# S5 scan in segments, S5 states copied to contiguous rows, rotary and value steps moved between engines

## The chip, the cores and the metric

The kernel runs on 1 core of one Trainium2 chip. The metric is the device time of one execution in microseconds (us); the time of a kernel is the median of its runs. The engines are named as the profile names them: PE (TensorE matmuls), PEld (its weight loads), DVE (VectorE), ACT (ScalarE), POOL (GpSimd) and SP (SyncE, which issues all loads and stores here).

## The reference, cut to what matters

Two transformer-like blocks work on one sequence of 512 positions and 1024 features in fp32. The change lies in the second block: a projection into q, k, v, two gates and u, eight heads of retention with rotary positions, and an S5 branch, a linear recurrence over the 512 positions with 64 groups of 64 complex states.

```python
def second_block(x, mem, positions, norm1_g, w_in, ret_gn_g, s5_a_re, s5_a_im, s5_log_dt,
              s5_b_re, s5_b_im, s5_c_re, s5_c_im, s5_d, s5_glu_w, s5_glu_b, w_out,
              norm2_g, norm_mem_g, xa_wq, xa_wk, xa_wv, xa_wo, norm_f_g):
...
        h = rms_norm(x, norm1_g[l])
        proj = h @ w_in[l]
        q, k, v, g_ret, u, g_s5 = jnp.split(proj, SPLITS, axis=-1)
        q = rotary(q.reshape(B, L, RET_HEADS, RET_DK), positions)
        k = rotary(k.reshape(B, L, RET_HEADS, RET_DK), positions)
        v = v.reshape(B, L, RET_HEADS, RET_DV)
        ret = retention(q, k, v, ret_gn_g[l]).astype(x.dtype) * jax.nn.silu(g_ret)
        ssm = s5_branch(u, s5_a_re[l], s5_a_im[l], s5_log_dt[l], s5_b_re[l], s5_b_im[l],
                        s5_c_re[l], s5_c_im[l], s5_d[l], s5_glu_w[l],
                        s5_glu_b[l]).astype(x.dtype) * jax.nn.silu(g_s5)
        x = x + jnp.concatenate([ret, ssm], axis=-1) @ w_out[l]
...
def s5_branch(u, a_re, a_im, log_dt, b_re, b_im, c_re, c_im, d, glu_w, glu_b):
...
    def combine(e1, e2):
        a1r, a1i, b1r, b1i = e1
        a2r, a2i, b2r, b2i = e2
        return (a2r * a1r - a2i * a1i,
                a2r * a1i + a2i * a1r,
                a2r * b1r - a2i * b1i + b2r,
                a2r * b1i + a2i * b1r + b2i)

    _, _, xr, xi = lax.associative_scan(combine, (a_seq_re, a_seq_im, bu_re, bu_im), axis=1)
    y = (jnp.einsum('blgn,gpn->blgp', xr, c_re.astype(f32))
         - jnp.einsum('blgn,gpn->blgp', xi, c_im.astype(f32)))
    y = y.reshape(Bsz, L, W) + d.astype(f32) * uf
    y = jax.nn.gelu(y)
    y = y * jax.nn.sigmoid(y @ glu_w.astype(f32) + glu_b.astype(f32))
    return y
```

`rotary` swaps the two halves of each head's 64 features and combines them with cosine and sine; `retention` has a per-head normalisation of the 128 value features, whose mean the kernel takes off v beforehand.

## The kernel before

**Tiles and passes.** Activations lie transposed, 128 features in the partitions and 512 positions in the columns, eight tiles (KT = 8) for 1024 features. Each fp32 product is made of three passes in a rounded fp32 form (fp32r), high by high, low by high and high by low part, so a 128 x 128 piece of a weight costs three 128x512 matmuls. A weight tile goes through SP (load into `wr`), ACT (high part `wh`) and DVE (`wl` = `wr` - `wh`), two tiles ahead of the matmuls that use it. PSUM has six buffers `ps` for products and two `st` for everything short. 61 SBUF slots of 128x512 (`s` in the trace) are handed out by `A()` and given back by `F()`.

**What sets the order.** `ft` and `tf` are the weight jobs. `n.later(cost, f)` puts a piece of work on a background queue, and a job's `pump=` says how much of the queue goes out in the course of the job; `delay` puts a step off by some jobs. From this program order a scheduler makes the queue of each engine.

**The stretch around the change, in order of time.** (1) u jobs; `state_in` multiplies u by input matrices and ACT writes the results into `arr` [128, 128 chunks, 2, 32]: 128 chunks of four positions; real and imaginary parts; 32 columns, so the 128 chunks of one column lie 256 bytes apart. (2) The scan over the chunks, `step(c)`, c = 1..127: four DVE operations of 64 columns, each on the result of chunk c - 1, sent by `later`. (3) Eight q/k jobs with `ev_qk`: four DVE copies of 32 partitions swap the halves, one DVE product, and a product and a sum on POOL. (4) Two v jobs with `ev_v`: scaled copy on ACT, mean over 128 columns on DVE, subtraction on POOL. (5) A loop over eight heads with two gate jobs each, scores, value products, normalisation. (6) `s5_load(m)`, `s5_out(m)`, m = 0..7: for four column groups a product with `M` and two with `Cr`, `Ci` whose moving operand is read from `arr` with its 256-byte step; ACT takes the sum out and SP stores it to `Yd`. They run among the weight matmuls of `w_out`. (7) `s5_act` and eight glu jobs. Earlier, about 830 to 1100 us, `small` and its neighbours make the S5 tables (powers of the transition, `s5P`) beside other weight jobs.

Two view helpers, `cj` and `jc`, read a 512-column tile as 4 x 128 and 128 x 4; one of the two walks in steps of 16 bytes.

## Time and profile before

| | us |
|---|---|
| median of 3 runs (1859.61 to 1868.07) | 1859.93 |
| the profiled execution | 1861.86 |
| its span | 1860.1 |

| engine | busy us | share |
|---|---|---|
| PE | 1796.9 | 97% |
| PEld | 1480.5 | 80% |
| DVE | 1250.5 | 67% |
| ACT | 654.6 | 35% |
| POOL | 360.4 | 19% |

A page of the profile tells how long each engine was busy and what it waited for; a timeline lists instructions in order of start, equal neighbours put together (x4), and in brackets the idle time ahead of one and who ended it. Matmuls overlap, so the price of one is the distance from start to start, not its length. The clock column of a stretch is the granted TensorE clock as a share of full speed.

### The profile page before, as it was taken

What the parts mean: (1) busy time and instruction counts of PE and PEld (TensorE: products, weight loads), DVE (VectorE), ACT (ScalarE), POOL (GpSimd) and SP (SyncE); (2) the same over time, 40 slices, a digit from 0 to 9 for tenths busy, and PEclk for the clock granted to TensorE, in tenths of its full rate; (3) what the DMA queues carried; (4) which work ended last, traced back from release to release, by engine and by line L of the source; (5) the groups of instructions that cost most, each with busy time, mean ns of one, the idle gap of its engine ahead of it and who ended that gap; (6) DMA issues with size and microseconds to landing.
All of it is one profiled execution on the core that took longest, in us unless ns stands there. A gap on an engine that the chain in (4) does not pass through costs nothing.

```text
span 1860.1 us, 22090 instructions
## 1 busy us (share of the span) xinstructions
PE 1796.9 (97%) x8242; PEld 1480.5 (80%) x8242; DVE 1250.5 (67%) x2242; ACT 654.6 (35%) x891; POOL 360.4 (19%) x316
## 2 busy tenths in 40 slices
PE   5999999999999998999998999999998999999997
PEld 4888888888877887788876888888876778888886
DVE  7888634478999999767443434476599993356644
ACT  4322223333387522424321222334322222354442
POOL 2000001130000000234436963024231010012102
PEclk9999999999999999999999999999998999999999
DMA  8788433233322223235656352454622225653211
GB/s 318 299 318 316 144 111 102 85 119 131 102 80 80 91 94 114 87 129 175 190 151 190 126 198 90 163 173 90 208 70 77 80 86 172 191 158 124 87 46 57
DMA packets 105356, 261.48 MB, mean 141 GB/s; under 512 B 15008, under 2 KB 32032, under 8 KB 105120
## 3 DMA queue, kind: packets, MB, share of 16 engines
q1 hardware_dynamic: 105248, 260.07, 42.6%
q8 instruction: 64, 1.05, 0.2%
q14 instruction: 44, 0.36, 0.1%
HBM read 239.19 MB, written 20.84 MB: 140 GB/s over the span
## 4 chain that ended last, share of the span: by engine, by line
PE 59%; issue 16%; DVE 11%; POOL 6%; DMA 6%; ACT 2%; SPq 1%; DVEq 0%; POOLq 0%; ACTq 0%
PE ps L152 54%; POOL s L133 5%; PE st L152 4%; DVE s L136 3%; DVE wl L133 2%; DVE arr L133 1%; DMA s<-Fd 1%; DVE s L133 1%; DVE st L133 1%; ACT s L147 1%; DMA wr<-in_ffn_w_gate 1%; DMA s<-in_s_bt_im 1%; DVE s L1464 1%; SPq L130 1%; DMA s<-in_s_bt_re 1%
## 5 line engine op out<-in xcount | busy, mean ns | idle before, releaser
L152 PE MATMUL ps<-s,wh 128*128 128x512 f32 (+1 forms) x4272 | 1321.0, 391 | 9.8 <-ACT wh L147 4.9
L152 PEld LDWEIGHTS ps<-s,wh 128*128 128x128 f32 x4272 | 800.5, 189 | 180.1 <-ACT wh L147 7.1
L152 PE MATMUL ps<-s,wl 128*128 128x512 f32 (+1 forms) x2136 | 830.6, 389 | 2.7 <-DVE wl L133 2.7
L147 ACT ACTIVATE wh<-wr 128x1024 fp32r<-128x1024 f32 (+1 forms) x277 | 289.5, 1047 | 834.1 <-PE ps L152 523.8
L133 DVE TENSOR_TENSOR wl<-wr,wh 128x1024 fp32r<-128x1024 f32 (+1 forms) x277 | 357.8, 1292 | 202.1 <-ACT wh L147 199.0
L152 PEld LDWEIGHTS ps<-s,wl 128*128 128x128 f32 x2136 | 402.3, 188 | 87.4 <-DVE wl L133 4.5
L133 POOL TENSOR_TENSOR s<-s,s 128x512 f32<-128x512 f32 (+2 forms) x168 | 232.6, 1389 | 708.0 <-DVE s L136 347.0
L133 DVE TENSOR_TENSOR s<-s,s 128x512 fp32r<-128x512 f32 (+3 forms) x249 | 199.3, 809 | 54.1 <-ACT s L147 52.5
L147 ACT ACTIVATE s<-s 128x512 fp32r<-128x512 f32 (+3 forms) x246 | 153.5, 637 | 224.7 <-DVE s L133 135.4
L152 PE MATMUL ps<-s,s 128*128 128x512 f32 (+7 forms) x648 | 152.5, 386 | 27.8 <-ACT s L147 19.3
L136 DVE SCALAR_TENSOR_TENSOR s<-s,ccw,s 128x503 f32<-128x503 f32 (+27 forms) x240 | 163.2, 735 | 0.7
L152 PEld LDWEIGHTS ps<-s,s 128*128 128x128 f32 (+2 forms) x648 | 108.4, 179 | 66.1 <-issue 22.7
L133 DVE TENSOR_TENSOR s<-s,ps 128x512 f32<-128x512 f32 (+1 forms) x61 | 40.7, 669 | 139.8 <-PE ps L152 139.6
L136 DVE SCALAR_TENSOR_TENSOR s<-ps,c,s 128x512 f32<-128x512 f32 x56 | 41.9, 748 | 83.5 <-PE ps L152 83.2
L389 DVE SCALAR_TENSOR_TENSOR ar<-ar,silc 128x1024 f32<-128x1024 f32 x72 | 89.2, 1251 | 10.2 <-DMA ar<-in_ada_w 9.7
L147 ACT ACTIVATE s<-ps 128x512 f32<-128x512 f32 (+1 forms) x115 | 66.2, 586 | 10.4 <-PE ps L152 10.3
L133 DVE TENSOR_TENSOR arr<-arr,st 128x64 f32<-128x64 f32 x254 | 63.2, 249 | 3.8
L133 DVE TENSOR_TENSOR s<-ps,s 128x512 f32<-128x512 f32 (+4 forms) x80 | 46.6, 615 | 24.6 <-PE ps L152 24.3
L133 DVE TENSOR_TENSOR s<-s,st 128x512 f32<-128x512 f32 x73 | 46.6, 680 | 14.4 <-PE st L273 13.9
L133 DVE TENSOR_TENSOR st<-arr,a 128x64 f32<-128x64 f32 x254 | 52.5, 245 | 3.6
L284 POOL TENSOR_TENSOR ls<-ls,mhalf 128x4 f32<-128x4 f32 x4 | 4.1, 1024 | 257.3 <-DVE ls L136 257.3
L133 POOL TENSOR_TENSOR s<-s 128x256 f32<-128x256 f32 x1 | 0.8, 846 | 246.8 <-ACT s L147 246.8
(155 smaller groups left out, 954.1 us busy)
## 6 DMA issues: line engine op xcount, KB each, us to landing
wr<-in_w_in SPq DMA_DIRECT2D x80, 512.0 KB
ar<-in_ada_w SPq DMA_DIRECT2D x72, 512.0 KB
wr<-in_ffn_w_gate SPq DMA_DIRECT2D x44, 512.0 KB
wr<-in_ffn_w_up SPq DMA_DIRECT2D x44, 512.0 KB
wr<-in_ffn_w_down SPq DMA_DIRECT2D x32, 512.0 KB
s<-Cd SPq DMA_DIRECT2D x32, 256.0 KB
wr<-in_w_out SPq DMA_DIRECT2D x16, 512.0 KB
wr<-in_ffn_w_down SPq DMA_DIRECT2D x16, 384.0 KB
```

Source lines behind the costliest of these rows:

```text
L130: self.nc.sync.dma_start(out=out, in_=in_)
L133: (eng or self.nc.vector).tensor_tensor(out=out, in0=a, in1=b, op=op)
L136: self.nc.vector.scalar_tensor_tensor(out=out, in0=a, scalar=s, in1=b, op0=op0, op1=op1)
L147: self.nc.scalar.activation(out=out, in_=in_, func=f, scale=scale)
L152: self.nc.tensor.matmul(out, lhsT=lhsT, rhs=rhs, start=start, stop=stop)
L284: self.nc.gpsimd.tensor_tensor(out=out, in0=v, in1=self.mhalf[:, 0:n], op=ALU.pow)
L389: n.nc.vector.scalar_tensor_tensor(out=w, in0=w, scalar=1.0, in1=n.silc, op0=ALU.mult, op1=ALU.mult, accum_out=n.mod[:, j:j + 1])
L1464: nc.vector.tensor_copy(out=s[b * 32:(b + 1) * 32], in_=ps[(b ^ 1) * 32:((b ^ 1) + 1) * 32])
```

## The change

The scan is done over 16 segments of eight chunks: seven steps inside all segments at once (in two halves of 512 columns), 15 short steps that carry the last chunk of one segment to that of the next, and seven steps that add the carried state to the other chunks (512 and 448 columns). Each step is four DVE operations with a slot as its temporary, so 508 operations become 172. The factors are powers 4, 8, .. 32 of the transition, made in `small` (`q4r`, `q4i`). `s5_load` copies the states of one m by two ACT operations into two slots with contiguous rows, and `s5_out` reads those, so an m holds six slots for four. The rotary copies go from DVE to ACT and the two POOL operations to DVE; the values' scaling, mean and subtraction are done by DVE from PSUM, without ACT and POOL. The pump amounts of the three kinds of jobs rise. `ccw` becomes a slot that is given back, and `mean_h` a column of `means`.

```diff
+    means = n.C([128, 2], name="means")
+    n.mean1, n.mean_h = means[:, 0:1], means[:, 1:2]
     nc.vector.memset(n.mean1, 1.0 / 1024)
+    nc.vector.memset(n.mean_h, 1.0 / 128)
...
-    n.ccw = n.C([128, 248], name="ccw")
-    n.ts(n.ccw, n.vecs[:, CCW_AT * 8:(CCW_AT + 31) * 8], 0.5)
+    n.ccw = n.A()
+    n.ts(n.ccw[:, 0:248], n.vecs[:, CCW_AT * 8:(CCW_AT + 31) * 8], 0.5)
...
+        n.F(n.ccw)
...
+        n.q4r, n.q4i = n.C([128, 8, 32], name="q4"), n.C([128, 8, 2, 32], name="q4i")
+        Q = n.q4r, n.q4i[:, :, 1, :]
+        for j in range(2):
+            nc.vector.tensor_copy(out=Q[j][:, 0, :], in_=P[j][:, 4, :])
+        s3 = n.A()
+        t3 = s3[:, 0:128].rearrange("p (k q) -> p k q", k=4)
+        for w in (1, 2, 4):
+            b = [Q[j][:, w - 1, :].unsqueeze(1).to_broadcast([128, w, 32]) for j in range(2)]
+            cmul(n, Q[0][:, w:2 * w, :], Q[1][:, w:2 * w, :], Q[0][:, 0:w, :], Q[1][:, 0:w, :], b[0], b[1], t3[:, 0:w, :])
+        n.F(s3)
+        n.ts(n.q4i[:, :, 0, :], Q[1], -1.0)
...
-        a8 = [n.C([128, 2, 32], name="a8") for _ in range(2)]
-        for j in range(2):
-            nc.vector.tensor_copy(out=a8[0][:, j, :], in_=n.s5P[0][:, 4, :])
-        n.ts(a8[1][:, 0, :], n.s5P[1][:, 4, :], -1.0)
-        nc.vector.tensor_copy(out=a8[1][:, 1, :], in_=n.s5P[1][:, 4, :])
-        G["a8"] = a8
-        G["tmp"] = [n.C([128, 2, 32], name="st") for _ in range(2)]
...
-            for c in range(1, 128):
-                n.later(0.55, step(c))
-
-    def step(c):
-        def f():
-            arr, a8, tmp = G["arr"], G["a8"], G["tmp"]
-            p = arr[:, c - 1]
-            n.tt(tmp[0], p, a8[0], ALU.mult)
-            n.tt(tmp[1], p[:, ::-1, :], a8[1], ALU.mult)
-            n.tt(arr[:, c], arr[:, c], tmp[0], ALU.add)
-            n.tt(arr[:, c], arr[:, c], tmp[1], ALU.add)
-        return f
+            scan()
+
+
+
+    def scan():
+        x = G["arr"].rearrange("p (s i) r q -> p s i r q", i=8)
+
+        def add(dst, src, i, w):
+            def f():
+                s = n.A()
+                t = s[:, 0:w * 64].rearrange("p (s r q) -> p s r q", s=w, r=2)
+                re = n.q4r[:, i].unsqueeze(1).unsqueeze(1).to_broadcast([128, w, 2, 32])
+                im = n.q4i[:, i].unsqueeze(1).to_broadcast([128, w, 2, 32])
+                n.tt(t, src, re, ALU.mult)
+                n.tt(dst, dst, t, ALU.add)
+                n.tt(t, src[:, :, ::-1, :], im, ALU.mult)
+                n.tt(dst, dst, t, ALU.add)
+                n.F(s)
+            return f
+
+        for i in range(1, 8):
+            for h in (slice(0, 8), slice(8, 16)):
+                n.later(2.8, add(x[:, h, i], x[:, h, i - 1], 0, 8))
+        for s in range(1, 16):
+            n.later(1.0, add(x[:, s:s + 1, 7], x[:, s - 1:s, 7], 7, 1))
+        for i in range(7):
+            for lo, hi in ((1, 9), (9, 16)):
+                n.later(2.8, add(x[:, lo:hi, i], x[:, lo - 1:hi - 1, 7], i, hi - lo))
...
+        for r in range(2):
+            x = n.A()
+            n.act(x.rearrange("p (a c) -> p a c", a=4), G["arr"][:, :, r, m * 4:m * 4 + 4].rearrange("p c a -> p a c"), AF.Copy)
+            t.append(x)
...
-        U, M, Cr, Ci = G.pop(("s5", m))
-        arr = G["arr"]
+        U, M, Cr, Ci, Xr, Xi = G.pop(("s5", m))
         ps = n.ST()
         for c in range(4):
             x = slice(c * 128, (c + 1) * 128)
             n.mm(ps[:, x], M[:, x], U[:, x], True, False)
-            for r, w in enumerate((Cr, Ci)):
-                n.mm(ps[:, c * 128 + 1:(c + 1) * 128], w[:, x], arr[:, 0:127, r, m * 4 + c], False, r == 1)
+            for r, (w, s) in enumerate(((Cr, Xr), (Ci, Xi))):
+                n.mm(ps[:, c * 128 + 1:(c + 1) * 128], w[:, x], s[:, c * 128:c * 128 + 127], False, r == 1)
         n.act(U, ps, AF.Copy)
         n.load(Yd[m], U)
-        n.F(U, M, Cr, Ci)
+        n.F(U, M, Cr, Ci, Xr, Xi)
...
             for b in range(4):
-                nc.vector.tensor_copy(out=s[b * 32:(b + 1) * 32], in_=ps[(b ^ 1) * 32:((b ^ 1) + 1) * 32])
+                n.act(s[b * 32:(b + 1) * 32], ps[(b ^ 1) * 32:((b ^ 1) + 1) * 32], AF.Copy)
             t = n.A()
             n.tt(t, ps, n.cos, ALU.mult)
-            n.tt(s, s, n.sin, ALU.mult, nc.gpsimd)
-            n.tt(t, t, s, ALU.add, nc.gpsimd)
+            n.tt(s, s, n.sin, ALU.mult)
+            n.tt(t, t, s, ALU.add)
...
-        n.ft([(w2[m], KT)], X, ev_qk(m), pump=0.6)
+        n.ft([(w2[m], KT)], X, ev_qk(m), pump=2.0)
...
-                n.act(v, pss[t], AF.Copy, scale=r1.r[:, t:t + 1])
                 mu = n.C([128, 4], name="mu")
-                v4 = v.rearrange("p (h e) -> p h e", h=4)
-                nc.vector.reduce_sum(out=mu, in_=v4, axis=AX.X)
-                n.ts(mu, mu, 1.0 / 128)
-                n.tt(v4, v4, mu.unsqueeze(2).to_broadcast([128, 4, 128]), ALU.subtract, nc.gpsimd)
+                ps4, v4 = (x.rearrange("p (h e) -> p h e", h=4) for x in (pss[t], v))
+                nc.vector.reduce_sum(out=mu, in_=ps4, axis=AX.X)
+                n.ts(mu, mu, r1.r[:, t:t + 1], 1.0 / 128, ALU.mult, ALU.mult)
+                n.stt(v4, ps4, r1.r[:, t:t + 1], mu.unsqueeze(2).to_broadcast([128, 4, 128]), ALU.mult, ALU.subtract)
...
-        tf(n, [a["w_v_2"][half, i] for i in range(4)], X, 4, ev_v(half), pump=2.0)
+        tf(n, [a["w_v_2"][half, i] for i in range(4)], X, 4, ev_v(half), pump=9.0)
...
-            n.ft([(w2[(8, 24)[j] + m], KT)], X, ev_g(j, m), pump=3.0)
+            n.ft([(w2[(8, 24)[j] + m], KT)], X, ev_g(j, m), pump=3.5)
```

DVE, at the second and third q/k job (`ps` a job's result, `s` slots, `st`, `a` and `arr` the scan's). Before:

```order
L133 TENSOR_TENSOR wl_9997<-wr_9994,wh_9996 128x1024
L1464 COPY s_10025<-ps_10000 32x512 x3
L133 TENSOR_TENSOR s_10030<-ps_10000,s_6465 128x512
L133 TENSOR_TENSOR wl_10055<-wr_10052,wh_10054 128x1024
L1464 COPY s_10083<-ps_10058 32x512 x4
L133 TENSOR_TENSOR s_10088<-ps_10058,s_6465 128x512
L133 TENSOR_TENSOR wl_10107<-wr_10104,wh_10106 128x1024
L133 TENSOR_TENSOR st_9520<-arr,a_9514 128x64
L133 TENSOR_TENSOR st_9521<-arr,a_9515 128x64
L133 TENSOR_TENSOR arr<-arr,st_9520 128x64
L133 TENSOR_TENSOR arr<-arr,st_9521 128x64
```

Now, at the third q/k job (`q` and `q4i` are the scan's new factors):

```order
L133 TENSOR_TENSOR wl_10122<-wr_10119,wh_10121 128x1024
L133 TENSOR_TENSOR s_10103<-ps_10073,s_6464 128x512
L133 TENSOR_TENSOR s_10098<-s_10098,s_6465 128x512
L133 TENSOR_TENSOR s_10159<-arr,q_6605 128x512
L133 TENSOR_TENSOR s_10103<-s_10103,s_10098 128x512
L133 TENSOR_TENSOR arr<-arr,s_10159 128x8x64
L133 TENSOR_TENSOR s_10204<-arr,q_6605 128x512
L133 TENSOR_TENSOR s_10159<-arr,q4i_6606 128x512
L133 TENSOR_TENSOR arr<-arr,s_10204 128x8x64
L133 TENSOR_TENSOR arr<-arr,s_10159 128x8x64
L133 TENSOR_TENSOR wl_10167<-wr_10164,wh_10166 128x1024
```

The copies are gone from this queue, product and sum of the rotary stand in it, and the scan, which begins after the third job's product in both, is made of operations 512 columns wide.

ACT, from the last head's split to the S5 outputs (`st` are S5 sums that go out, `arr` the states). Before:

```order
L147 ACTIVATE s_11893<-s_11724 128x512
L147 ACTIVATE s_12001<-st_12025 128x512
L147 ACTIVATE s_12009<-st_12048 128x512
L147 ACTIVATE s_12070<-s_11882 128x512
L147 ACTIVATE s_12040<-st_12082 128x512
L147 ACTIVATE s_12074<-st_12105 128x512
```

Now:

```order
L147 ACTIVATE s_11696<-s_11561 128x512
L147 ACTIVATE s_11723<-arr 128x512
L147 ACTIVATE s_11725<-arr 128x512
L147 ACTIVATE s_11735<-arr 128x512
L147 ACTIVATE s_11737<-arr 128x512
L147 ACTIVATE s_11770<-arr 128x512
L147 ACTIVATE s_11772<-arr 128x512
L147 ACTIVATE s_11808<-arr 128x512
L147 ACTIVATE s_11715<-st_11747 128x512
L147 ACTIVATE s_11810<-arr 128x512
```

Seven copies of states stand ahead of the first sum, where before the first sums followed one another.

PE, first S5 output (`ps` with `wh`, `wl` is `w_out`; `st` the S5 sum). Before:

```order
L152 MATMUL st_12025<-s_12001,s_12002 128x128
L152 MATMUL ps_12195<-s_11262,wh_11741 128x512
L152 MATMUL ps_12195<-s_11261,wl_11742 128x512
L152 MATMUL st_12025<-arr,s_12003 128x127
L152 MATMUL ps_12195<-s_11419,wh_11741 128x512
L152 MATMUL ps_12195<-s_11420,wh_11741 128x512
L152 MATMUL ps_12195<-s_11419,wl_11742 128x512
L152 MATMUL st_12025<-arr,s_12004 128x127
L152 MATMUL st_12025<-s_12001,s_12002 128x128
L152 MATMUL st_12025<-arr,s_12003 128x127
L152 MATMUL st_12025<-arr,s_12004 128x127
```

Now:

```order
L152 MATMUL ps_12014<-s_11046,wh_11643 128x512
L152 MATMUL ps_12014<-s_11047,wh_11643 128x512
L152 MATMUL ps_12014<-s_11046,wl_11644 128x512
L152 MATMUL ps_12014<-s_11190,wh_11643 128x512
L152 MATMUL ps_12014<-s_11191,wh_11643 128x512
L152 MATMUL st_11747<-s_11723,s_11717 128x127
L152 MATMUL st_11774<-s_11727,s_11728 128x128
L152 MATMUL st_11747<-s_11725,s_11718 128x127
L152 MATMUL st_11747<-s_11715,s_11716 128x128
L152 MATMUL st_11747<-s_11723,s_11717 128x127
L152 MATMUL st_11747<-s_11725,s_11718 128x127
```

The second operand comes from a slot instead of `arr`, and 15 weight matmuls, of which the last five are shown, stand between the first product with M and the first with the states, where before there were two.

## Rows read from the trace of the kernel before

**Rows 1.** Page, first part: busy time, share of span, instructions of each engine.
```profile
PE 1796.9 (97%) x8242; PEld 1480.5 (80%) x8242; DVE 1250.5 (67%) x2242; ACT 654.6 (35%) x891; POOL 360.4 (19%) x316
```

**Rows 2.** Stretches: length, busy PE, PEld, DVE, ACT, POOL, clock, DMA share, GB/s.
```profile
1324.00:1367.75 43.75, 43.75 (x219) 37.08 (x217) 39.65 (x65) 11.76 (x15) 18.73 (x12) 1.00 0.26 90
1367.75:1419.98 52.23, 47.87 (x193) 38.03 (x192) 50.07 (x158) 13.20 (x16) 12.94 (x9) 0.93 0.24 81
1419.98:1453.86 33.88, 27.50 (x106) 19.92 (x104) 32.23 (x128) 6.90 (x9) 4.16 (x4) 0.85 0.25 86
1453.86:1565.97 112.11, 112.11 (x506) 86.09 (x506) 91.64 (x324) 33.28 (x48) 10.77 (x7) 1.00 0.29 95
1565.97:1606.08 40.11, 40.10 (x219) 37.54 (x218) 4.90 (x7) 6.40 (x10) 1.01 (x1) 1.00 0.65 211
```

**Rows 3.** Timeline, PE: start, length, instructions, idle before and its releaser.
```profile
1365.71 0.61 PE L152 MATMUL ps<-s,wh 128*128 128x512 f32 x2
...
1366.39 0.61 PE L152 MATMUL ps<-s,wh 128*128 128x512 f32 x2
...
1376.13 0.50 PE L152 MATMUL ps<-wl,s 128*128 128x512 f32 x1 [1.82 <-DVE wl L133]
...
1407.84 0.50 PE L152 MATMUL ps<-wl,s 128*128 128x512 f32 x1 [2.33 <-DVE wl L133]
...
1439.98 4.60 PE L152 MATMUL ps<-s,s 128*128 128x512 f32 x8 [6.38 <-DVE s L133]
```

**Rows 4.** Timeline, PE: 128-column matmuls from contiguous rows, then from the state array.
```profile
1315.34 7.48 PE L152 MATMUL st<-s,s 128*128 128x128 f32 x64
1322.57 0.47 PE L152 MATMUL ps<-s,wl 128*128 128x512 f32 x1
...
1583.78 1.03 PE L152 MATMUL st<-arr,s 128*128 128x127 f32 x4
1584.63 0.40 PE L152 MATMUL st<-s,s 128*128 128x128 f32 x2
```

**Rows 5.** Timeline, DVE, in the q/k jobs and in the first head round.
```profile
1366.71 1.81 DVE L133 TENSOR_TENSOR wl<-wr,wh 128x1024 fp32r<-128x1024 f32 x1
1368.45 1.44 DVE L133 TENSOR_TENSOR st<-arr,a 128x64 f32<-128x64 f32 x2
...
1370.32 0.36 DVE L133 TENSOR_TENSOR st<-arr,a 128x64 f32<-128x64 f32 x2
...
1440.74 1.21 DVE L133 TENSOR_TENSOR wl<-wr,wh 128x1024 fp32r<-128x1024 f32 x1
```

**Rows 6.** Timeline, POOL, beside the first of those.
```profile
1366.15 3.52 POOL L133 TENSOR_TENSOR s<-s,s 128x512 f32<-128x512 f32 x2 [3.78 <-DVE s L1464]
```

**Rows 7.** Groups by shape, DVE, 1287 to 1570: count, busy us, mean ns.
```profile
L133 DVE TENSOR_TENSOR arr<-arr,st 128x64 f32<-128x64 f32 x254 | 63.2, 249 | 3.8
L133 DVE TENSOR_TENSOR st<-arr,a 128x64 f32<-128x64 f32 x254 | 52.5, 245 | 3.6
...
L1464 DVE COPY s<-ps 32x512 f32<-32x512 f32 x32 | 22.0, 687 | 16.7 <-PE ps L152 16.2
L1486 DVE TENSOR_REDUCE mu<-s 128x4 f32<-128x512 f32 x8 | 5.4, 678 | 0.0
```

**Rows 8.** Timeline, DVE: 512 contiguous columns, then 512 with 16-byte steps (`jc`, `cj`).
```profile
1289.64 1.29 DVE L133 TENSOR_TENSOR s<-s,s 128x512 f32<-128x512 f32 x2
1290.85 4.94 DVE L133 TENSOR_TENSOR s<-ps,s 128x512 f32<-128x512 f32 x5
```

**Rows 9.** Groups by shape, ACT, 1287 to 1570, then 1606 to 1640.
```profile
L147 ACT ACTIVATE arr<-st 128x512 f32<-128x512 f32 x16 | 9.6, 597 | 18.9 <-PE st L152 18.9
...
L147 ACT ACTIVATE s<-s 128x512 f32<-128x512 f32 x8 | 9.0, 1122 | 10.5 <-DVE s L136 10.5
...
L147 ACT ACTIVATE s<-st 128x512 f32<-128x512 f32 x1 | 0.6, 598 | 3.5 <-PE st L152 3.5
```

**Rows 10.** Timeline, PE, while the S5 tables are made.
```profile
1014.62 0.73 PE L152 MATMUL ps<-s,wh 128*128 128x512 f32 x2 [2.63 <-ACT wh L147]
```

More of the change, by code (lines that the diff above doesn't have):

```diff
@@ L373, in setup @@
     nc.vector.memset(n.ones_est, 1.0 / (128 * LN.EST))
-    n.mean1 = n.C([128, 1], name="mean1")
+    means = n.C([128, 2], name="means")
+    n.mean1, n.mean_h = means[:, 0:1], means[:, 1:2]
     nc.vector.memset(n.mean1, 1.0 / 1024)
+    nc.vector.memset(n.mean_h, 1.0 / 128)
     n.mhalf = n.C([128, 32], name="mhalf")
@@ L1318, in second_block @@
     r1 = Rms(n)
-    n.mean_h = n.C([128, 1], name="meanh")
-    nc.vector.memset(n.mean_h, 1.0 / 128)
     Ud = n.DT([8, 2, 4, 64, 128], "Ud")
```

## The prediction

> **What bounds the kernel now.** I read the page first: PE is busy for 97% of the span [rows 1], so a change counts only where it takes work from PE, takes a stall from PE, or makes one. The 512-column matmuls follow one another at 0.68 us for three, 0.227 each [rows 3]; that is the floor of the weight jobs. Then I read the stretches of the second block one by one [rows 2]. In three of them PE is full (q/k jobs, later head rounds, S5 outputs); in the v jobs (52.23 us) and in the 33.88 us behind them it is not, and the clock column falls to 0.93 and 0.85. The v jobs hold 192 matmuls: 192 x 0.227 = 43.6, so 8.6 us are lost. Their timeline shows where [rows 3]: PE waits 1.82 and 2.33 us for `wl`, a weight's low part from DVE, and runs on slowly. In the first head round it waits 6.38 us for DVE, and the eight matmuls behind that take 4.60 us where eight at the steady rate take 1.8: 6.4 + 2.8 = 9.2. Together 17.8 us.
>
> Why DVE is late: it is busy 39.65 of 43.75, 50.07 of 52.23 and 32.23 of 33.88 us [rows 2]. It carries the scan (508 operations, 115.7 us), 22.0 us of rotary copies [rows 7], and it is slowed while POOL works: beside a POOL pair of 3.52 us [rows 6] `wl` takes 1.81 us and two scan operations 1.44, alone 1.21 and 0.36 [rows 5]. In the later head rounds DVE has slack again (91.64 of 112.11).
>
> The last place is the S5 outputs. There PE is full, yet its work is dear: 64 matmuls of 128 columns from contiguous rows take 1322.57 - 1315.34 = 7.23 us, 0.113 each; four from `arr`, with its 256-byte step, take 1584.63 - 1583.78 = 0.85, 0.2125 each [rows 4].
>
> **S5 operands contiguous.** 128 instructions go from 0.2125 to 0.113: 128 x 0.0995 = **-12.7 us**, all on PE, in a stretch in which PE never waits. The DMAs stay: at 211 GB/s and a share of 0.65 over 40.1 us [rows 2] they would take 0.65 x 40.1 = 26 us at full share, against 27.4 us that the stretch then has, so loads are about to bind too and cover less.
>
> **The copies that pay for it.** Sixteen ACT copies read `arr` with the step. No row shows this very operation. From below: ACT spread 512 columns from PSUM into `arr` in 0.597. From above: the GELU of `s5_act`, which writes in 16-byte steps, takes 1.122 [rows 9]. ACT has room for either (6.40 us of 40 used), but its order puts seven copies ahead of the first S5 sum and four more ahead of the second, while there are two `st` buffers, so the normalisation's next product waits for the first sum and the third S5 output for the second. The copies also need the whole scan: eight of its wide operations stand behind the last gate job's `wl`, near the start of the S5 outputs, and the 15 weight matmuls that now stand there cover all but about 1 us.
> - At 1.12: the first sum is out 7 x 1.12 + 0.6 = 8.4 us after the scan. PE begins after two copies (2.2) and has two outputs of 24 x 0.113 = 2.7 to do, so it is through at 7.6 and waits 0.8. The second sum is out at 8.4 + 4 x 1.12 + 0.6 = 13.5, PE is there at about 9.5: 4 us. With 1 us for the scan and some 2 us of slow matmuls behind such a wait (the 2.8 above is one case), 8 us.
> - At 0.60: sums at 4.8 and 7.8, PE through at 6.6 and 7.2: under 1 us, with the scan's wait 2 us.
>
> I take **+6**: the upper price is nearer by its kind of access, SBUF in small steps, but weight matmuls may fill part of the wait. So this half of the change is worth about -7.
>
> The Trainium skill ("SBUF — State Buffer", Specifications) says that SBUF is read in 16-byte lines and that each cross to a new line pays a penalty, which speaks against the copies: the step does not go away, ACT walks it now. The matmul prices of [rows 4] agree with it. By the page the copies cost like the GELU and the term is +8; without it +2.
>
> **Rotary, values and scan.** What leaves DVE: 32 copies, 22.0 us, and 508 narrow operations, 115.7 us [rows 7]. What comes: 16 operations for the rotary and 8 for the values at 0.645 (512 contiguous columns, 1.29 for two [rows 8]), 15.5 us; the scan in 112 wide operations at 0.645 and 60 narrow at 0.18 [rows 5], 72 + 11 = 83 us. POOL's q/k and v work goes away, and with it the slow `wl`. But more of the scan is pumped early: 56 of the 112 wide operations now lie before the end of the v jobs. DVE then has there: 56 x 0.645 = 36, 24 new operations 15.5, 21 `wl` at 1.21 = 25, the products of the eight q/k jobs 5, eight reductions of 0.678 [rows 7] and their small steps about 7: 89 us against 87.3 us of PE (43.75 + 43.6). So DVE is about as full as PE, no longer behind by 17.8. What lateness is left is covered by the two weight tiles that are prepared ahead (2 x 24 x 0.227 = 10.9 us). I take a rest of **+2** (0 to 5) and so **-15.8** in place of -17.8. ACT gets 32 copies: at about 0.6 each 19 us on top of 11.76 in 43.75 us; it keeps room. In the head rounds the rest of the scan, about 56 wide and 55 narrow operations, 46 us, takes the place of what was left of the old one; PE kept full there with DVE at 91.64 of 112.11.
>
> **Small edits.** The new table operations (24 against 4) are short, some 4 us of DVE at about 840 us, where PE has other weight jobs. But two hundred us later PE does wait on weights whose loads stand behind the tables' loads on SP (2.63 us at 1014.62 [rows 10], and a like one before): shifts of that order may move it either way. I take **0**, -3 to +5. `ccw` as a slot and `means` cost nothing: neither lies on a wait. The glu jobs begin sooner after the last S5 output and may wait for `s5_act`: 0, up to +2.
>
> **The sum.** 1861.86 - 12.7 + 6 - 15.8 + 0 = 1839.4 for the profiled execution. It stood 1.93 us above the median, so the forecast is about **1838 us**.
>
> **Rivals.**
> - *The copies cost the lower price and the ring hides them*: +2 instead of +6, 1834. For it: PSUM read with a step cost ACT nothing extra (0.597). Chance 0.14.
> - *Not the step makes the matmuls of `arr` dear*, but what stays, their 127 columns or the output that begins one column late. Then -12.7 is gone, and with it most of the wait for copies, PE being slower: 1838 + 12.7 - 4 = 1847. Against it: the two kinds differ in the operand above all. 0.08.
> - *DVE stays the bound.* The wide operations read segments 2 KB apart, one operand repeated, one reversed. If they cost what 512 columns in 16-byte steps cost, 4.94 for five = 0.99 [rows 8], the 56 early ones add 56 x 0.345 = 19 us of DVE, and with the 2 us it was behind PE loses what it loses now: 1861.86 - 1.9 - 12.7 + 6 - 17.8 + 21 = 1856, no change. Against it: inside a segment 64 columns are contiguous, and the narrow operation has the same reversal at 0.18. 0.10.
> - *Slower: the same place at a higher price.* To come out over 0.5% slower the stalls there must reach 34 us, so 32 us more on 56 operations, 0.57 each: from 1.22 us per wide operation. The nearest thing would be that each of the eight 64-column pieces costs like a narrow operation, 8 x 0.18 = 1.44; then 56 x 0.8 = 45 and 1861.86 - 1.9 - 12.7 + 6 - 17.8 + 47 = 1882. Nothing in the rows shows such a price per piece. 0.05.
> - *A new stall of over 10 us elsewhere* (tables, slots, six per m now): 1852 or so. 0.05.
>
> **How the numbers follow.** The forecast has 0.58. The best ends of all terms together: -12.7 + 2 - 17.8 - 3 = -31.5, 1828; the worst without a rival: -12.7 + 8 - 17.8 + 5 + 5 + 2 = -10.5, 1850. From 1829 to 1850 lie the forecast and the first two rivals, 0.80. This kernel can be told from no change at about 0.5%, so faster means under 1850.6: 0.80; within: 0.15; slower: 0.05.
>
> **What the profile will show.** S5: matmuls from slots at 0.113 each; copies of `arr` between 0.6 and 1.12 on ACT, with PE waits for them in the first three outputs only. Q/k and v: clock column 1.00, DVE about 90% busy, `wl` at 1.2 throughout, wide operations at 0.65. If the wide operations stand at 1.0 and PE waits for `wl`, the third rival holds. The forecast fails if matmuls from slots stay at 0.21, if the scan ends so late that the copies start well after the first product with M, or if the table stretch loses more than 5 us.

## The result

The changed kernel took 1841.97 us (median of 4 runs, 1838.59 to 1847.32) against 1860.72 before (4 runs): 18.75 us less, faster by 1.0%, a ratio of 0.9898 with a 95% interval of 0.988 to 0.9916. The forecast was 1838, the range 1829 to 1850. Its profiled execution happened to be the slowest of the four, 1847.32 us with a span of 1845.5.

### The profile page after: what moved, and what is told of

Read it like the earlier page. It is cut to its first block, busy times and chain, and to the rows that moved or that the text cites. A ratio compares the mean times of both kernels' runs of the same rounds, so it can differ in the third digit from the quotient of the medians.

```text
span 1845.5 us, 21756 instructions
## 1 busy us (share of the span) xinstructions
PE 1784.5 (97%) x8242; PEld 1469.6 (80%) x8242; DVE 1219.0 (66%) x1915; ACT 682.9 (37%) x931; POOL 322.7 (17%) x292
## 4 chain that ended last, share of the span: by engine, by line
PE 78%; POOL 7%; DMA 6%; DVE 4%; ACT 2%; issue 2%; SPq 1%; DVEq 0%; POOLq 0%; ACTq 0%
PE ps L152 75%; POOL s L133 6%; PE st L152 3%; DMA s<-in_s_bt_im 2%; DVE s L133 1%; ACT s L147 1%; SPq L130 1%; DMA s<-in_s_bt_re 1%; DVE ar L391 1%; DVE s L136 1%; DMA wr<-in_ffn_w_down 1%; DMA s<-Fd 1%; DMA wr<-in_ffn_w_gate 1%; DVE wl L133 0%; POOL s L143 0%
## 5 line engine op out<-in xcount | busy, mean ns | idle before, releaser
L152 PE MATMUL ps<-s,wh 128*128 128x512 f32 (+1 forms) x4272 | 1324.3, 392 | 11.7 <-ACT wh L147 6.6
L133 DVE TENSOR_TENSOR wl<-wr,wh 128x1024 fp32r<-128x1024 f32 (+1 forms) x277 | 354.2, 1279 | 210.9 <-ACT wh L147 205.6
L133 POOL TENSOR_TENSOR s<-s,s 128x512 f32<-128x512 f32 (+2 forms) x152 | 202.5, 1337 | 632.1 <-DVE s L136 326.0
L133 DVE TENSOR_TENSOR s<-s,s 128x512 fp32r<-128x512 f32 (+2 forms) x265 | 205.5, 783 | 55.4 <-ACT s L147 54.3
L136 DVE SCALAR_TENSOR_TENSOR s<-s,s,s 128x503 f32<-128x503 f32 (+26 forms) x240 | 164.1, 745 | 0.7
L147 ACT ACTIVATE s<-ps 128x512 f32<-128x512 f32 (+2 forms) x147 | 85.3, 588 | 15.5 <-PE ps L152 15.0
L284 POOL TENSOR_TENSOR gs<-gs,mhalf 128x4 f32<-128x4 f32 x8 | 11.0, 1371 | 259.6 <-DVE gs L141 259.6
L152 PE MATMUL st<-s,s 128*128 128x127 f32 (+2 forms) x368 | 51.5, 297 | 4.4 <-ACT s L147 3.1
L152 PEld LDWEIGHTS st<-s,s 128*128 128x128 f32 x368 | 47.9, 197 | 8.1 <-ACT s L147 3.6
L133 DVE TENSOR_TENSOR s<-s,st 128x512 f32<-128x512 f32 x73 | 46.6, 681 | 11.5 <-PE st L273 11.1
```

The costliest lines, as they stand in the source:

```text
L133: (eng or self.nc.vector).tensor_tensor(out=out, in0=a, in1=b, op=op)
L136: self.nc.vector.scalar_tensor_tensor(out=out, in0=a, scalar=s, in1=b, op0=op0, op1=op1)
L147: self.nc.scalar.activation(out=out, in_=in_, func=f, scale=scale)
L152: self.nc.tensor.matmul(out, lhsT=lhsT, rhs=rhs, start=start, stop=stop)
L284: self.nc.gpsimd.tensor_tensor(out=out, in0=v, in1=self.mhalf[:, 0:n], op=ALU.pow)
```

## The profile after

The page, first part (busy us, share of the span, instructions; before: [rows 1]): DVE has 327 instructions fewer but only 31.5 us less to do.

```profile
PE 1784.5 (97%) x8242; PEld 1469.6 (80%) x8242; DVE 1219.0 (66%) x1915; ACT 682.9 (37%) x931; POOL 322.7 (17%) x292
```

Both kernels hold 8242 matmuls, and up to the S5 outputs in the same order save eight of them at 849 us. So the start of the k-th matmul can be compared between two traces, and the difference tells where time is won or lost. The table is worked out in that way (us; negative is gained). "Again" is a second profile of the changed kernel, from a later run.

| part of the program | forecast | after | again |
|---|---|---|---|
| up to the end of the S5 tables (1108 us) | 0 (-3 to +5) | +8.7 | +5.6 |
| q/k jobs, v jobs, first head round | -15.8 | -17.7 | -17.7 |
| other head rounds | 0 | +1.3 | -0.3 |
| S5 outputs | -6.7 | -7.0 | -6.5 |
| the rest | 0 (to +2) | +0.2 | -0.1 |
| sum | -22.5 | -14.5 | -19.0 |

Stretches of the changed kernel (length, busy PE, PEld, DVE, ACT, POOL, clock, DMA share, GB/s): q/k jobs, v jobs, first head round, other head rounds, S5 outputs. They answer to [rows 2].

```profile
1331.00:1374.60 43.60, 43.60 (x220) 37.07 (x219) 32.45 (x46) 28.78 (x44) 0.00 (x0) 1.00 0.31 106
1374.60:1418.10 43.50, 43.50 (x193) 36.03 (x193) 43.10 (x74) 10.86 (x12) 0.00 (x0) 1.00 0.31 104
1418.10:1445.00 26.90, 26.90 (x115) 20.37 (x115) 16.29 (x35) 6.88 (x9) 0.00 (x0) 0.99 0.25 83
1445.00:1558.00 113.00, 113.00 (x503) 86.66 (x502) 86.43 (x171) 32.27 (x46) 9.59 (x7) 0.99 0.29 94
1558.00:1592.70 34.70, 30.34 (x217) 28.02 (x218) 8.59 (x14) 21.98 (x26) 1.38 (x1) 0.95 0.78 259
```

The v jobs take 43.50 us, their 192 matmuls at 0.227, and POOL is at 0.00 through the first three. DVE is still busy for 43.10 of 43.50 us, and yet PE waits for nothing. In the S5 outputs PE is busy for 30.34 of 34.70 us: the matmuls are cheap now and something else ends last. The DMA share went from 0.65 to 0.78.

The 1.3 us lost in the other head rounds are the clock: from 1444.6 to 1448.0 us it stood at half, behind eight matmuls of one column and without a wait. The second profile runs the same matmuls there at the full clock and loses nothing. The stretch, in the columns of the last fence:

```profile
1444.60:1448.00 3.40, 3.40 (x9) 2.61 (x9) 3.02 (x15) 0.00 (x0) 1.01 (x1) 0.51 0.62 210
```

What PE waits for from the q/k jobs to the glu jobs, the largest line of its waits (us in all, times, longest):

```profile
PE st L152 <- ACT s L147: 3.1, 1, 3.1
```

The timeline of PE in the S5 outputs (start, length, instruction, idle before):

```profile
1565.33 5.15 PE L152 MATMUL st<-s,s 128*128 128x128 f32 x44 [0.48 <-DMA s<-Ud]
...
1574.52 15.19 PE L152 MATMUL st<-s,s 128*128 128x128 f32 x120 [3.13 <-ACT s L147]
```

The 44 matmuls from slots at 1565.33 end their row in 5.15 us, 0.113 apart, both kinds alike: the step was what made those of [rows 4] dear. Then PE waits 3.13 us for ACT. The timeline of ACT shows for what:

```profile
1562.58 7.04 ACT L147 ACTIVATE s<-arr 128x512 f32<-128x512 f32 x7 [2.91 <-DVE arr L133]
1569.52 0.58 ACT L147 ACTIVATE s<-st 128x512 f32<-128x512 f32 x1
1570.00 3.99 ACT L147 ACTIVATE s<-arr 128x512 f32<-128x512 f32 x4
1573.88 0.58 ACT L147 ACTIVATE s<-st 128x512 f32<-128x512 f32 x1
```

Seven copies from the end of the scan on, the first sum, four copies, the second sum: the third output starts when that is out, at 1574.46. Groups of ACT by shape (count, busy us, mean ns), beside [rows 9]:

```profile
L147 ACT ACTIVATE s<-ps 32x512 f32<-32x512 f32 x32 | 18.9, 590 | 3.3 <-PE ps L152 2.9
L147 ACT ACTIVATE s<-arr 128x512 f32<-128x512 f32 x16 | 16.4, 1083 | 3.8 <-DVE arr L133 2.9 <-DMA Yd<-s 0.9
```

Groups of DVE by shape, beside [rows 7, 8]:

```profile
L133 DVE TENSOR_TENSOR wl<-wr,wh 128x1024 fp32r<-128x1024 f32 x39 | 47.6, 1224 | 11.1 <-ACT wh L147 8.4 <-PE st L152 2.4
...
L133 DVE TENSOR_TENSOR arr<-arr,s 128x512 f32<-128x512 f32 x42 | 28.4, 687 | 0.1
L133 DVE TENSOR_TENSOR s<-arr,q 128x512 f32<-128x512 f32 x21 | 14.4, 687 | 0.1
```

A copy costs 1.083 us, near the upper bound of 1.12; a wide scan operation 0.687; `wl` 1.224 throughout.

Where the 8.7 us up to 1108 us come from: the timeline of DVE ahead of the second layer norm. `q` and `q4i` are the scan's factors, `ls` the layer norm's statistics.

```profile
837.16 1.28 DVE L133 TENSOR_TENSOR s<-q4i,q 128x32 f32<-128x32 f32 x1
838.37 0.21 DVE L133 TENSOR_TENSOR q<-q 128x64 f32<-128x64 f32 x1
...
841.55 0.74 DVE L136 SCALAR_TENSOR_TENSOR s<-ps,c,s 128x512 f32<-128x512 f32 x1
...
850.40 0.15 DVE L136 SCALAR_TENSOR_TENSOR ls<-ls 128x4 f32<-128x4 f32 x1
```

And the timeline of PE behind it:

```profile
852.15 0.65 PE L273 MATMUL st<-ident,ls 128*128 128x128 f32 x4 [2.42 <-POOL ls L284]
...
875.26 0.74 PE L152 MATMUL ps<-s,wh 128*128 128x512 f32 x2 [0.80 <-ACT wh L147]
877.07 0.50 PE L152 MATMUL ps<-s,wl 128*128 128x512 f32 x1 [1.07 <-DVE wl L133]
```

Between 836.2 and 842.5 us DVE does 17 of the 21 factor operations among those that the layer norm needs (the other four were done at 210 us). In the kernel before, PE waited 0.49 us at the same product with `ls`, here 2.42, then 0.80 and 1.07 for the weights behind it, and then the clock fell to half for 3.4 us (the same columns once more):

```profile
878.00:881.40 3.40, 3.40 (x10) 2.63 (x9) 0.99 (x2) 0.87 (x1) 0.00 (x0) 0.50 0.98 258
```

From 848 to 880 us this adds up to +4.9 us. Of the rest, 0.7 us were lost before 848 us, ahead of these operations, and 3.0 between 880 and 1108 us, where PE waits for weights that stand behind the tables' loads, as in [rows 10].

## Experiments

Each kernel was run beside the kernel before; ratios are to that, with 95% intervals. Terms in us come from the same comparison of matmul starts.

### The changed kernel again

No edit.

> The changed kernel, timed and profiled once more, as the measure for the others on the same chip. Theory 1 (the 5 us that PE loses at 849 to 880 us and the 3.5 us more up to 1108 come from the factor operations that stand ahead of the second layer norm on DVE): the losses are there again within 1 us, time 1842 to 1847. Rival (they are chance of one execution, since the profiled one was the slowest of four): the stretch up to 1108 us loses 2 us or less against before, time about 1839.

Ratio 0.9897 (0.9882 to 0.9912), median 1842.88. PE waits 2.42 us at the layer norm again, and 3.3 us are lost between 848 and 880 us; the clock doesn't fall there this time, and that is the difference to 4.9:

```profile
852.99 0.65 PE L273 MATMUL st<-ident,ls 128*128 128x128 f32 x4 [2.42 <-POOL ls L284]
```

So that loss belongs to the change. The part from 880 to 1108 us came to +0.8 instead of +3.0: that part differs from run to run.

### The factors at the start of the second block

```diff
     def small():
-        n.q4r, n.q4i = n.C([128, 8, 32], name="q4"), n.C([128, 8, 2, 32], name="q4i")
...
     def begin():
...
         G["arr"] = n.arr
+        n.q4r, n.q4i = n.C([128, 8, 32], name="q4"), n.C([128, 8, 2, 32], name="q4i")
...
```

> The factors of the scan are computed at the start of the second block instead of in the S5 tables; nothing else differs from the changed kernel. Theory 1: the wait for the second layer norm's statistics at 849 us falls from 2.4 back to about 0.5 us and the whole stretch to 1108 us to within 2 us of before, 5 to 9 us faster than the changed kernel, 1833 to 1837. Rival (the slots that turn differently, through the freed slot of the convolution's weights, make the losses): same time as the changed kernel within 2 us.

Ratio 0.9879 (0.9863 to 0.9896), median 1841.40: less gained than theory 1 asked for, and not told from the changed kernel by the intervals. The trace says why. The loss at 848 to 880 us is gone (+0.0), but 3.7 us are lost between 880 and 1108 us, and between 1104 and 1320 us 3.9 us that the changed kernel doesn't lose. The scheduler put the operations into the third layer norm, and PE waits there. DVE's timeline:

```profile
1279.28 1.23 DVE L133 TENSOR_TENSOR q<-q,s 128x32 f32<-128x32 f32 x1
...
1281.78 1.33 DVE L133 TENSOR_TENSOR q4i<-q4i,s 128x32 f32<-128x32 f32 x1
...
1283.29 1.30 DVE L133 TENSOR_TENSOR q4i<-q,q4i 128x64 f32<-128x64 f32 x1
...
1286.05 0.68 DVE L133 TENSOR_TENSOR s<-s,s 128x512 fp32r<-128x512 f32 x1
```

PE, at the end of the same layer norm:

```profile
1286.78 3.42 PE L152 MATMUL ps<-s,s 128*128 128x512 f32 x8 [2.97 <-DVE s L133]
```

POOL, beside the factor operations:

```profile
1279.16 1.29 POOL L133 TENSOR_TENSOR s<-s,s 128x512 f32<-128x512 f32 x1
...
1281.75 4.09 POOL L133 TENSOR_TENSOR s<-s,s 128x512 f32<-128x512 f32 x3
```

Of the factor operations, some 0.2 us each alone, four take 1.2 to 1.3 us here, where POOL works too; each of the four ends within 0.1 us of the end of a POOL operation. The last high-low split of the layer norm's output stands behind them at 1286.05, and PE waits 2.97 us for it. The wait goes where the factors go.

### Copies shared between ACT and DVE

In `s5_load`, with the factors at the start of the second block:

```diff
-            n.act(..., AF.Copy)
+            if r:
+                nc.vector.tensor_copy(out=o, in_=v)
+            else:
+                n.act(o, v, AF.Copy)
```

> Factors late as in the run with the late tables, and of the two state copies of one m the imaginary one on DVE, which is nearly idle there. Theory 1 (PE's wait of 3.1 us in the S5 outputs is the second sum standing behind eleven ACT copies): the wait falls under 1 us, and the time is 2 to 4 us below the run with late tables, 1831. Rival (loads and the ring of two sums bind anyway, DMA share 0.78 there): within 1 us of the run with late tables.

Ratio 0.9874 (0.9855 to 0.9893), median 1837.12: 23.7 us under the kernel before beside it (1860.85), where the run with late tables was 21.5 under its own (1862.85). The intervals of the two overlap, so the time alone doesn't tell them apart; the trace does. PE's wait for ACT shrinks to 0.3 us, and the S5 outputs gain 11.7 us in place of 7.3. At the third layer norm this run loses 5.8 us, 1.9 more than the run with late tables. The group of DVE's copies (count, busy us, mean ns):

```profile
L1440 DVE COPY s<-arr 128x512 f32<-128x512 f32 x8 | 5.9, 765 | 10.5 <-DMA Yd<-s 6.7 <-PE st L152 3.8
```

The group of copies on ACT:

```profile
L147 ACT ACTIVATE s<-arr 128x512 f32<-128x512 f32 x8 | 8.6, 1104 | 4.4 <-DVE arr L133 2.9 <-PE st L152 1.0 <-ACT s L147 0.4
```

Waits of PE for the S5 sums:

```profile
PE st L152 <- DMA s<-Cd: 0.7, 1, 0.7
...
PE st L152 <- ACT s L147: 0.3, 1, 0.3
```

The same copy takes 0.765 us on DVE and 1.104 on ACT.

### The sums taken out by DVE

```diff
-        n.act(U, ps, AF.Copy)
+        nc.vector.tensor_copy(out=U, in_=ps)
```

> Factors late, the state copies all on ACT, but the S5 sums are taken out by DVE. Theory 1: the sums no longer stand behind copies, PE's wait of 3.1 us goes, 2 to 4 us below the run with late tables. Rival (the copies themselves come too late for the third and later S5 outputs, at 1.08 each two per output against 2.7 us of PE): PE waits for copies instead, within 1 us of the run with late tables.

Ratio 0.9876 (0.9856 to 0.9897), median 1837.81, again not told from the run with late tables by the intervals; S5 outputs -11.8 us with all sixteen copies on ACT. PE no longer waits for ACT there, only once 1.5 us for a load. So sixteen copies at 1.09 us on one engine are early enough; what cost time was that the sums stood behind them.

### Shared copies, the factors behind the u jobs

```diff
+        if m == 0:
+            powers(U)
         n.F(U, Br, Bi)
```

Beside the shared copies: `powers` holds the factor operations, and their temporary is the slot of the first state product, so they can't start before it.

> The run with split copies, but the scan's factors wait for the first state product, so that they stand behind the u jobs on DVE and ahead of no layer norm. Theory 1 (the loss goes where the factors go): the 5.8 us that the run with split copies lost between 1104 and 1320 us shrink to under 1.5, ratio 0.984, 1831 to 1834. Rival (the loss there belongs to the other slots or to chance): still 4 to 6 us lost there, 1837.

Ratio 0.986 (0.9841 to 0.9879), median 1835.96. Nothing is lost at 848 to 880 us, and 0.0 us between 1104 and 1320. This run lost 3.3 us between 876 and 1104 us. But so does the last run below, which has the old scan and no factors (4.4), while the one ahead of it, the same there, lost 1.2: that stretch is not the factors' and moves by such amounts. Theory 1 holds for the 4.9 and 3.3 us at the layer norm; that the 3.0 behind them belong to the change is not shown.

### The states read with their step

`s5_load` and `s5_out` of the kernel before in the changed kernel.

```diff
-                n.mm(ps[:, c * 128 + 1:(c + 1) * 128], w[:, x], s[:, c * 128:c * 128 + 127], False, r == 1)
+                n.mm(ps[:, c * 128 + 1:(c + 1) * 128], w[:, x], arr[:, 0:127, r, m * 4 + c], False, r == 1)
```

> The changed kernel with S5 outputs that read the state array in steps of 256 bytes as before, so without the copies. Theory 1: 7 us slower than the changed kernel (12.7 less some 6 given back), about 1849; matmuls from the array at 0.2125. Rival (the copies give back nearly all): within 2 us of the changed kernel.

Ratio 0.9934 (0.9914 to 0.9954), median 1848.24: 7 us more than the changed kernel by the ratios (0.0037 x 1860). Matmuls from the array, timeline of PE:

```profile
1575.47 1.03 PE L152 MATMUL st<-arr,s 128*128 128x127 f32 x4
1576.32 0.40 PE L152 MATMUL st<-s,s 128*128 128x128 f32 x2
```

0.85 us for four again; S5 outputs +0.4 in place of -7.0.

### The copies alone

`s5_load` and `s5_out` of the changed kernel in the kernel before.

```diff
         n.load(t[3], n.Cd[m, 1])
+        for r in range(2):
+            x = n.A()
...
+            t.append(x)
```

> The kernel before with the states copied to contiguous rows and nothing else of the change. The old scan ends some 30 us before the S5 outputs, so the copies can't wait for it. Theory 1 (the matmuls gain 12.7 us and 3 to 7 are given back because two S5 sums wait behind copies on ACT): 6 to 10 us faster than before, 1851 to 1855, with copies at 1.08 each. Rival A (what is given back comes from the late end of the new scan): copies are done early and all of 12 to 13 us is gained, 1848. Rival B (copies steal slots and SP's loads come late): under 4 us gained.

Ratio 0.9952 (0.9937 to 0.9967), 8.7 us less by the medians. The old scan is long done, and copies begin ahead of the outputs; PE's waits for ACT come to 1.6 us in two. From 1445 us on the kernel gains 8.0: theory 1's size, but with half the wait, so rival A has a part. Of the 1.6 us, 1.2 lie ahead of the S5 outputs, where the last head's results, which ACT takes out of PSUM, stand behind copies. Waits of PE in the second block:

```profile
PE ps L152 <- DVE s L133: 6.5, 2, 6.3
PE ps L152 <- DVE wl L133: 4.3, 3, 2.3
PE st L152 <- ACT s L147: 1.6, 2, 1.2
```

The waits for DVE in the q/k, v and first head jobs are those of [rows 3], untouched.

### The moves alone

`ev_qk` and `ev_v` of the changed kernel in the kernel before; old scan, old pump amounts.

```diff
-            n.tt(s, s, n.sin, ALU.mult, nc.gpsimd)
-            n.tt(t, t, s, ALU.add, nc.gpsimd)
+            n.tt(s, s, n.sin, ALU.mult)
+            n.tt(t, t, s, ALU.add)
...
-                n.act(v, pss[t], AF.Copy, scale=r1.r[:, t:t + 1])
...
+                n.stt(v4, ps4, r1.r[:, t:t + 1], mu.unsqueeze(2).to_broadcast([128, 4, 128]), ALU.mult, ALU.subtract)
```

> The kernel before with the rotary copies on ACT, the POOL work of rotary and values on DVE, old scan, old pump amounts, old S5 operands. Theory 1 (POOL beside DVE and the 22 us of copies made DVE late; DVE then has about 122 - 22 + 15 - 10 = 105 us for 112 us of PE): 13 to 17 us faster than before, 1844 to 1848, no wait of PE for a weight's low part in the value jobs. Rival (the many short scan operations made DVE late): under 6 us faster, the 6.4 us wait in the first head round still there.

Ratio 0.9908 (0.9893 to 0.9922), median 1844.96. All of the 17.7 us are gained in the q/k, v and first head jobs, and PE's waits for DVE there come to 0.2 us. The scan is the old one.

### The scan in segments alone

The changed kernel with `ev_qk`, `ev_v` and the S5 outputs of before, factors at the start of the second block.

```diff
-            for c in range(1, 128):
-                n.later(0.55, step(c))
+            scan()
...
-        n.ft([(w2[m], KT)], X, ev_qk(m), pump=0.6)
+        n.ft([(w2[m], KT)], X, ev_qk(m), pump=2.0)
...
```

> The kernel before with the scan in segments and the new pump amounts; factors made at the start of the second block; rotary, values and S5 operands as before. Theory 1 (POOL's work and the copies make DVE late, and the scan, pumped earlier, adds to it): no gain or a loss, 1858 to 1868, PE waiting for DVE in the value jobs. Rival (fewer, wider scan operations are what frees DVE): 10 to 17 us faster, 1843 to 1850.

Ratio 0.999 (0.9977 to 1.0002): no difference that can be measured. In the q/k, v and first head jobs it gains 9.0 us, half of what the moves gain; 7.6 were lost ahead of them, 4.4 of these at the third layer norm with the factors. So neither side had it whole: the segments do relieve DVE, and the factors that they need take half of it back; the other 3.2 us fall into the stretch up to 1108 us that differs from run to run.

### The rotary copies alone on ACT

```diff
-                nc.vector.tensor_copy(out=s[b * 32:(b + 1) * 32], in_=ps[(b ^ 1) * 32:((b ^ 1) + 1) * 32])
+                n.act(s[b * 32:(b + 1) * 32], ps[(b ^ 1) * 32:((b ^ 1) + 1) * 32], AF.Copy)
```

> The kernel before with the rotary copies on ACT and nothing else: POOL keeps its work. Theory 1a (the 22 us of copies alone made DVE late): nearly all of the gain of the moves, 13 to 17 us, 1845. Theory 1b (POOL's work beside DVE, which slows it, matters as much): 6 to 11 us, 1850 to 1855. Rival: under 3 us.

Ratio 1.0013 (1.0001 to 1.0024): nothing gained, though 22 us of copies left DVE. The rival's number came true, and theory 1a as it stands is out. Groups of DVE of this run, the scan's (1287 to 1570 us):

```profile
L133 DVE TENSOR_TENSOR arr<-arr,st 128x64 f32<-128x64 f32 x254 | 67.8, 267 | 3.9
L133 DVE TENSOR_TENSOR st<-arr,a 128x64 f32<-128x64 f32 x254 | 53.3, 247 | 4.1 <-ACT arr L147 0.4
```

Groups of POOL, the rotary and the values:

```profile
L133 POOL TENSOR_TENSOR s<-s,s 128x512 f32<-128x512 f32 x16 | 21.5, 1353 | 80.5 <-ACT s L147 57.7 <-DVE arr L133 12.1 <-DVE st L133 5.3
...
L133 POOL TENSOR_TENSOR s<-s,mu 128x512 f32<-128x512 f32 x8 | 8.4, 1047 | 43.9 <-DVE mu L141 36.7 <-DVE st L133 4.9 <-issue 2.3
```

Waits of PE from the q/k jobs on:

```profile
PE ps L152 <- DVE wl L133: 7.0, 4, 2.4
PE ps L152 <- DVE s L133: 6.7, 1, 6.7
```

The groups of DVE of the run with the moves alone:

```profile
L133 DVE TENSOR_TENSOR arr<-arr,st 128x64 f32<-128x64 f32 x254 | 56.3, 222 | 3.9
L133 DVE TENSOR_TENSOR st<-arr,a 128x64 f32<-128x64 f32 x254 | 46.9, 221 | 3.6
L133 DVE TENSOR_TENSOR wl<-wr,wh 128x1024 fp32r<-128x1024 f32 x37 | 45.1, 1222 | 9.1 <-ACT wh L147 6.3 <-PE st L152 2.4
```

With POOL at work a scan operation takes 267 and 247 ns in the mean, without it 222 and 221. The mean hides that few are hit: in the kernel before 494 of the 508 take under 0.3 us and 14 take 0.9 to 1.4, each of these beside a POOL operation. I summed, for each run, by how much each DVE instruction from the first q/k job to the first head round exceeds the shortest of its shape, and set beside it what PE loses there against the 106.2 us of the changed kernel:

| run | DVE instructions slowed by, us | PE loses, us |
|---|---|---|
| before | 20.2 | 18.2 |
| rotary copies alone on ACT | 23.4 | 19.5 |
| scan in segments alone | 15.5 | 8.6 |
| moves alone | 2.3 | 0.0 |
| changed kernel | 0.7 | 0.0 |

Where no DVE instruction is slowed PE loses nothing, with the old scan or the new. The segments alone stand between: half is lost with three quarters of the slowing.

But the run with the copies alone moved does not show that less work on DVE is worth nothing, since its DVE did not get less. The scheduler filled the time with scan operations that ran later before. The scan's operations on DVE in the same stretch (length, busy DVE, clock, DMA share, GB/s), before, with the copies alone moved, and with the moves alone:

```profile
1324.00:1453.86 129.86, 62.10 (x268) 0.93 0.25 85
1324.17:1455.34 131.17, 81.08 (x341) 0.96 0.25 83
1324.50:1436.18 111.68, 49.81 (x271) 1.00 0.30 98
```

22.0 us of copies went and 73 scan operations, 19.0 us, came. The run with the moves alone has as many as before. So amount of work and slowing are not separated by these two runs. An estimate for the v jobs from the busy times, with the slowing summed as in the table: DVE's work without its slowing comes to 40 us before (50 less 10), 40 with the copies alone moved (51 less 11), 43 with the segments alone (48 less 5) and 40 with the moves alone (41 less 1), all under PE's 43.6. By it the slowing is what tips the balance. POOL's work moved with the copies left on DVE was not run, so that the slowing alone would do is argued, not shown.

### Moves and copies, old scan

The kernel before with the edits of the run with the moves alone and of the run with the copies alone:

```diff
+            n.tt(s, s, n.sin, ALU.mult)
...
+                n.mm(ps[:, c * 128 + 1:(c + 1) * 128], w[:, x], s[:, c * 128:c * 128 + 127], False, r == 1)
```

> The kernel before with the moves (rotary copies to ACT, POOL's rotary and value work to DVE) and the copied states, but with the old scan of 127 steps and the old pump amounts. Theory 1 (the two gains add and the scan in segments contributes nothing): -17 and -8.5 us together, ratio 0.986, 1835. Rival (the scan in segments is needed once DVE holds the rotary work, or the gains overlap): 1841 or more, as the changed kernel.

Ratio 0.9875 (0.9851 to 0.99), median 1838.97; the profiled execution has a span of 1833.6. Q/k to first head round -17.7, S5 outputs -11.1. Here too 1.4 us are lost just ahead of the S5 outputs, where the last head's results stand behind copies on ACT:

```profile
1549.77 1.05 PE L152 MATMUL st<-meanh,s 128*128 128x1 f32 x8 [1.23 <-ACT s L147]
```

So from the other head rounds on, this kernel gains 9.8 us, where the changed kernel gains 5.2 (with the loss at 1444.6 us in it) and 6.3 in its two profiles and the run with the copies alone 8.0. The gains add, and nothing is lost without the segments.

### Moves and shared copies, old scan

The same, with the imaginary copies on DVE:

```diff
+            if r:
+                nc.vector.tensor_copy(out=o, in_=v)
```

> The same with the imaginary state copies on DVE. Theory 1: 2 to 3 us less again, since in the run with the copies alone PE waited 1.6 us for ACT's sums and ran slowly behind that: ratio 0.984 to 0.985, 1832, the lowest of all. Rival (with the old scan the copies are early enough): within 1 us of the run before it.

Ratio 0.9853 (0.9829 to 0.9876), median 1835.44, the lowest of all: 26.5 us under the kernel before beside it, where the changed kernel was 18.8 and 20.0 under its own, and the changed kernel's interval lies above in both of its timings (0.988 to 0.9916, 0.9882 to 0.9912). Against the run before it the intervals overlap, and from the other head rounds on it gains 10.9 us for 9.8, so the shared copies add little that can be told here. Set beside its like with the new scan, the run with shared copies and the factors behind the u jobs (0.9841 to 0.9879), it is not told apart either. So beside the moves the scan in segments brings nothing that these runs can show; that the change is faster without it isn't shown by itself, as this run also differs from the changed kernel in its shared copies.

## Why the prediction was right, and where it wasn't

**What bounds the kernel.** Right in its places: PE's losses in the v jobs and the first head round, and dear matmuls in the S5 outputs. All 17.7 us of the first came back, and [rows 3] has no counterpart after. What the account calls running slowly is the clock, and it is about a third of that loss. PE in the kernel before, behind the first of the waits of [rows 3] and behind the third (length, busy PE, clock, DMA share, GB/s):

```profile
1377.50:1380.90 3.40, 3.40 (x10) 0.50 0.37 134
1439.98:1445.80 5.82, 5.82 (x12) 0.50 0.40 135
```

With a like stretch at 1408.2 us behind the second wait, 12.6 us pass at half the clock, 6.3 us lost; without the waits the column stays at 1.00 and 0.99.

**S5 operands and copies.** Right in mechanism and size: matmuls at 0.113, copies at 1.083, the first sum behind seven and the second behind four, a wait of 3.13 us where 4 was worked out, -7.0 for -6.7. What the forecast didn't weigh is the alternative: the copies start when the scan ends, and the sums' 8.4 and 13.5 us were counted from there. With the old scan, ended early, the same copies give back 2.9 us beside the moves (12.7 - 9.8) and 4.7 without them (12.7 - 8.0), in the changed kernel 5.7 (12.7 - 7.0). The sums taken out by DVE give back 0.9 (12.7 - 11.8) even with the new scan. The step that the Trainium skill's rule on 16-byte lines ("SBUF — State Buffer", Specifications) speaks of cost ACT 1.08 to 1.10 against 0.60; on DVE 0.765 against 0.69, a difference between engines that the rule doesn't make.

**Rotary, values and scan.** The term was right (-17.7 for -15.8), its account only in part. I had made a balance of DVE's work, with 22 us of copies and the scan's 115.7 us as the main entries, and POOL's slowing beside them. The run with the moves alone shows that the old scan could stay. The run with the copies alone moved shows that copies off DVE are worth nothing by themselves, because the scan takes their place. The balance leaves out that the scan fills whatever is free, and it gives least room to the entry that by the estimate above tips it: DVE instructions slowed by POOL, [rows 5, 6]. The Trainium skill has that rule ("SBUF — State Buffer", Who interferes with whom: a DVE instruction with two SBUF inputs contends with a GpSimd instruction that reads SBUF); the 20.2 us of slowing before, and 0.7 after, agree with it, and so does where the slowing lies: on `wl` and the scan, which read both inputs from SBUF, and not on the 32 copies out of PSUM, which stand 0.3 us over their shortest in all. A DVE that is busy for 43.10 of 43.50 us without a wait of PE shows too that a full DVE alone is no sign of a loss.

**Small edits.** This is the step that failed: "some 4 us of DVE at about 840 us, where PE has other weight jobs" at 0, -3 to +5. It was about that (17 operations there, 5.1 us added up), but the layer norm's chain stood behind it on the same engine, PE's next products wait for that, and in one of two profiles the clock fell behind the waits: 3.3 and 4.9 us. Up to 1108 us it came to +5.6 and +8.7, so the forecast's own sign of failure, over 5 us lost in the table stretch, appeared, though from 848 us on it is 4.1 and 8.0. The time stayed within the range because the range had room for it. Without this row of the table the two profiles gained 23.2 and 24.6 us, where the sum said 22.5.

**Rivals.** Wide operations at 0.687 put both DVE rivals out; the matmuls at 0.113 the one on the step. "A new stall elsewhere" of over 10 us did not come; a smaller one did, at the layer norm. The sum itself ends at 1837.4, which was written as about 1838.

## What to carry to other kernels

Before counting the work that leaves an engine, compare each of its instructions with the quickest of its shape: if they are stretched while another engine runs, try stilling that engine. Before you trust work moved off an engine, look whether the scheduler has filled the time with other work: here 73 scan operations took the place of 32 copies. Setup work costs what stands behind it on its engine, not what the other engines do meanwhile; look for the next chain that needs that engine, at the place where the order puts it. When two parts of a change share one gain, run each alone: here the part with the longest code showed no gain of its own.

## What was not expected of the hardware

ACT reads 512 columns at a step of 256 bytes from SBUF in 1.08 to 1.10 us and DVE the same in 0.765. For a copy of 512 contiguous columns out of PSUM they took 0.597 (the S5 sums on ACT) and 0.691 (the same on DVE, in the run that moved them). So the step seems to cost ACT about 0.5 us and DVE under 0.1, though the two copies differ in where they read as well, and DVE is the quicker engine for the copy with the step. And a short DVE operation that meets POOL loses most: of nine of 32 to 64 columns, about 0.2 us alone, four took 1.2 to 1.3 us at 1279 to 1285 us in the run with late factors, each up to the end of a POOL operation. The granted clock fell to half behind some waits of PE of a microsecond or two and not behind others: after the same 0.8 and 1.07 us at 875 to 878 us it fell in one profile of the changed kernel and stayed in the other.
